# A decoder trunk on one core: queries' parts from one SBUF copy, a filler step behind bare scores, block sums held and spread, first splits in fixed order

## The chip, the core and the metric

The kernel runs on one core of a Trainium2 chip. TensorE (PE in the profile) multiplies, VectorE (DVE) and ScalarE (ACT) here read the PSUM banks into which TensorE writes and write SBUF, GpSimd (POOL) here works from SBUF to SBUF, and SyncE (SP) issues the DMA transfers. Each engine works through its own instructions in order and waits on semaphores for the others. The metric is the device time of one execution in microseconds. A wait of TensorE is named by the instruction that ended it.

## The reference

Two layers act on 1024 tokens of 1024 features, in fp32. Each layer has two token mixers side by side and then a gated feed-forward part with a short causal convolution:

```python
for l in range(DEPTH):                                   # DEPTH = 2
    h = rmsnorm(x, norm1[l])
    proj = h @ w_in[l]                                   # q, k, v of both mixers and the gates
    qa, ka, va, qb, kb, vb, gate_pre = jnp.split(proj, splits, axis=-1)
    o_a = dilated_mixture(hd4(qa, 12), hd4(ka, 12), hd4(va, 12))    # dilated windows, ALiBi, softmax
    o_b = stick_breaking_attention(hd4(qb, 4), hd4(kb, 4), hd4(vb, 4))
    gates = jax.nn.sigmoid(gate_pre + b_gate[l])
    merged = g_a * (o_a @ w_br[l, :OUT_A]) + g_b * (o_b @ w_br[l, OUT_A:])
    x = x + merged @ w_o[l]
    h2 = rmsnorm(x, norm2[l])
    up = h2 @ w_up[l]                                    # 1024 x 5632
    a, v = up[..., :D_FF], up[..., D_FF:]
    a = causal_depthwise_conv(a, conv_w[l], conv_b[l])
    x = x + (jax.nn.gelu(a, approximate=False) * v) @ w_down[l]
return rmsnorm(x, norm_f)
```

Stick-breaking attention of query t over earlier keys s is `sigmoid(z_ts)` times the product of `1 - sigmoid(z_tj)` over the keys j between them. The dilated mixer has three groups of four heads (window 128 at dilation 1, 512 at 4, 2048 at 16), joined by their softmax denominators.

## The kernel before

**Products in parts.** Each operand of a product is split into a rounded high part and the rest. `split` (L128) makes a pair: ScalarE casts the high part (L129), VectorE subtracts it from the source (L130). A product is then three matmuls: high by high, high by low, low by high (L155 to L157). Nearly every operand that reaches TensorE has a pair of L129 and L130 behind it, weights (`w_hi`, `w_lo`) and activations alike.

**Seven products in place of eight.** The large projections (the gates, the dilated groups' keys, queries and values, the feed-forward part) are done by a Strassen-like scheme on 2 x 2 blocks. For it, sums of blocks of the normalised activations are needed in parts: S[1], S[2], S[3] in `t_hi`, `t_lo`, and S[4] in the place of a block of `hh`, `hl`. `block_sums` (L911) writes them as a list of small steps: `first` is three subtractions and additions on POOL (L928 to L930), `further` two on VectorE (L937, L938), `in_two` a split. Each step has a condition, a set of names that must be done first.

**The order of work.** TensorE's instructions stand exactly in the order in which the program writes them (`manual_schedule`, L1870). For the other engines a planner with a model of durations chooses the order within the bounds of the data: when an engine is free in its model it takes the ready instruction that was written first, and so it draws later work ahead of its place if nothing earlier is ready. `high_priority` makes it take an instruction as though it had been written 200 places earlier; the parts of attention weights (`parts`, L593) have it.

**Attention with fillers.** `attend` (L312) walks over a list of items: sixteen of the stick-breaking mixer (B00 to B17), four of the near group (N00 to N11) and sixteen of the two dilated ones (T00 to T17). An item has score steps (TensorE writes `z`, VectorE and ScalarE make weights of it) and pairs of a turn (TensorE transposes the weights, `parts` splits them) and an apply (TensorE multiplies the parts with the values). The steps of one item are mixed with the scores of the next; the last apply of an item, `late`, is written behind the first turn of the next one. Behind each step stands `dense.advance(rate)`: it draws one step of the side list (`aside`, L229) if its condition holds, adds `rate` to a counter, and for each whole one draws a filler, `dense.step()`: six matmuls of a projection. Scores that are left over at an item's end, or that had to wait for their inputs, are written bare, behind one another, each with its `advance`.

The side list holds the block sums. All that is left of it is written at once when the first unit of the seven-product kind is taken up (L262). Keys, queries and values are units of fillers too: `queries_half` (L532) multiplies into a PSUM bank `q_ps`, from which ScalarE takes the high parts of two heads (`qt`, L538; a DMA copies them to the other 64 partitions) and VectorE the low parts (`ql`, L543 and L544). Two banks with the tag `ps` serve all fillers by turns, and two with the tag `s` all scores.

**The opening.** `first` (L1821) loads token blocks of 128 rows, scales them by the norm, transposes them and splits the result into `hh`, `hl`. Between the blocks stand the first projections (`head`, L569): the values' weights come in four loads of 256 KB through two buffers (`wr`), each followed by its split. `masks` (L77) and five small loads (`setup`, L1852) are written ahead of the second block.

**The convolution.** In the feed-forward part `gated` (L1373) makes products of blocks j = 0 and 1; differences of them are taken on POOL (L1382), split and stored (`spill`). The second block's stand between the first ones of the seven-product units `up` (L1489), whose weights are loaded by the same SP queue.

Of the kernel before, what the change touches and what calls it, by code (L numbers as in the profile page):

```python
# [44 lines left out]
AHEAD = 200  # L45

# [6 lines left out]
def trunk_kernel(ctx, tc, x, norm1, w_in, b_gate, w_br, w_o, norm2, w_up, conv_w, conv_b, w_down, norm_f, out, depth=None, probe=None):  # L53
# [74 lines left out]
    def split(hi, lo, src):  # L128
        act.copy(hi, src)  # L129
        dve.tensor_tensor(lo, src, f32(hi), ALU.subtract)  # L130


    def weights(src, cols, place=None):
# [4 lines left out]
        for r in range(0, KD, per):  # L138
            raw = sb.tile([P, per, cols], F32, tag="wr", bufs=NRAW, name="w_raw")
# [55 lines left out]
    class Dense:  # L195
# [58 lines left out]
        def step(self):  # L254
            while True:
                if self.now is None:
# [4 lines left out]
                    if self.now[2] and not self.started:  # L261
                        while self.side:  # L262
                            n = len(self.side)
                            self.aside()
                            assert len(self.side) < n, (self.side, self.done)
# [46 lines left out]
    def attend(dense, items):  # L312
# [4 lines left out]
        for i, (name, first, rest, rate, make) in enumerate(items):  # L317
# [251 lines left out]
    def head(l):  # L569
# [6 lines left out]
        wv = weights(w_in[l][:, OFF_VB : OFF_VB + 256], 256, place(2, "v_w"))  # L576
# [334 lines left out]
    def block_sums(made):  # L911
# [20 lines left out]
        def further(t, a, i):  # L932
# [4 lines left out]
            dve.tensor_tensor(r, f32(ah), r, ALU.subtract)  # L937
            dve.tensor_tensor(r, r, f32(al), ALU.add)  # L938
# [13 lines left out]

        def series(after, t, f, lag, gap):
            steps = {}
            for i in range(4):
                steps.setdefault(i * gap, []).append(lambda i=i: f(i))
                steps.setdefault(i * gap + lag, []).append(lambda i=i: in_two(t, i))
            plan(after, steps)
# [52 lines left out]
    def pair_rest(dense, l, offs, put, view, grid, kept):  # L1011
# [13 lines left out]
        def run():  # L1025
# [47 lines left out]
            yield  # L1073
            for word in seven(pa, w4, S[4], False, True):
# [247 lines left out]
    def ffn(l, pending, final):  # L1322
# [50 lines left out]
        def gated(j, n, v):  # L1373
# [7 lines left out]
            def less(dst, a, b):  # L1381
# [515 lines left out]
```

## Time and profile before

| | |
|---|---|
| median of three runs | 2701.89 us (2699.85 to 2702.15) |
| profiled execution | 2703.52 us |
| its span | 2701.8 us |
| TensorE busy | 2650.5 us (98%) |
| VectorE busy | 2115.7 us (78%) |
| ScalarE busy | 1314.3 us (49%) |
| GpSimd busy | 734.9 us (27%) |
| mean granted clock of TensorE | 0.996 |

The span runs from the first to the last instruction; the profiled execution's own time is 1.7 us longer. An engine's busy time leaves out its waits. Where rows show "[1.28 <-DVE p0l L130]", the engine had been idle for 1.28 us and the instruction of VectorE that writes `p0l` at line 130 released it. Matmuls overlap, so that what a row of several takes is read from the starts.

### The profile page before, as it was taken

To read this page: it belongs to the slowest core of one execution; us is meant where nothing else is said; L and a number is where in the kernel's file an instruction comes from. 1 tells how busy PE (TensorE), PEld (TensorE's weight loads), DVE (VectorE), ACT (ScalarE), POOL (GpSimd) and SP (SyncE) were. 2 spreads that over 40 slices of the span, in tenths; PEclk is the share of its full clock that TensorE was granted. 3 is DMA by queue.
4 is the path that set the end of the run, shared out by engine and by line. 5 is a ranking of instruction groups with operands and counts; after the bars stand their busy time and mean duration, and the time that the engine had idled before them with its cause. 6 is when DMAs were issued, how large, how long until landed. Compare 5 with 4: busy or idle time off the path is not lost. (4 is left out here: it accounts for less than half of the span.)

```text
span 2701.8 us, 37158 instructions
## 1 busy us (share of the span) xinstructions
PE 2650.5 (98%) x13098; PEld 2226.4 (82%) x13098; DVE 2115.7 (78%) x3170; ACT 1314.3 (49%) x2434; POOL 734.9 (27%) x531
## 2 busy tenths in 40 slices
PE   8999999999999999999999999999999999999999
PEld 7888888888888888888889878888788888888888
DVE  5888876675789988897658887766858888998865
ACT  5656544364455555432335655434635555554225
POOL 2004133222233434321120042332311433343210
PEclk9999999999999999999999999999999999999999
DMA  4134489863235444688401334988732443447963
GB/s 153 28 97 125 132 239 234 205 229 118 82 117 172 141 156 143 222 325 313 167 32 48 102 120 145 254 208 226 234 90 75 151 160 135 170 144 254 333 246 121
DMA packets 399559, 448.88 MB, mean 166 GB/s; under 512 B 22044, under 2 KB 319372, under 8 KB 397836
## 3 DMA queue, kind: packets, MB, share of 16 engines
q1 hardware_dynamic: 399372, 446.49, 51.9%
q8 instruction: 104, 1.70, 0.3%
q14 instruction: 83, 0.68, 0.1%
HBM read 300.61 MB, written 142.67 MB: 164 GB/s over the span
## 5 line engine op out<-in xcount | busy, mean ns | idle before, releaser
L130 DVE TENSOR_TENSOR w_lo<-up_a,w_hi 128x512 fp32r<-128x512 f32 x240 | 236.9, 993 | 22.5 <-ACT w_hi L129 22.5
L129 ACT CAST w_hi<-up_a 128x512 fp32r<-128x512 f32 x240 | 149.4, 623 | 186.0 <-PE u_a L906 45.8
L1651 DVE TENSOR_TENSOR x<-x,d_ps 128x512 f32<-128x512 f32 (+1 forms) x228 | 152.3, 672 | 78.0 <-PE d_ps L1645 77.0
L1382 POOL TENSOR_TENSOR cv<-cv 128x512 f32<-128x512 f32 x88 | 131.9, 1509 | 249.0 <-DVE cv L1377 139.1
L130 DVE TENSOR_TENSOR w_lo<-w_raw,w_hi 128x512 fp32r<-128x512 f32 x176 | 133.9, 763 | 64.9 <-ACT w_hi L129 62.3
L129 ACT CAST w_hi<-w_raw 128x512 fp32r<-128x512 f32 x176 | 109.1, 621 | 130.1 <-PE o_ps L156 60.2
L129 ACT CAST w_hi<-in_a 128x512 fp32r<-128x512 f32 x140 | 86.8, 620 | 148.8 <-PE i_a L906 83.4
L130 DVE TENSOR_TENSOR g<-cv,g 128x512 fp32r<-128x512 f32 x154 | 152.3, 990 | 5.2 <-ACT g L129 2.8
L1643 PE MATMUL d_ps<-gd_in,w_hi 128*128 128x512 f32 (+1 forms) x340 | 130.2, 383 | 1.5 <-ACT w_hi L129 1.2
L1645 PE MATMUL d_ps<-gd_in,w_lo 128*128 128x512 f32 (+1 forms) x340 | 129.8, 382 | 0.0
L1644 PE MATMUL d_ps<-gd_in,w_hi 128*128 128x512 f32 (+1 forms) x340 | 129.7, 382 | 0.0
L905 PE MATMUL u_a<-hh,w_hi 128*128 128x512 f32 x320 | 124.7, 390 | 2.7 <-DVE u L1533 2.7
L906 PE MATMUL u_a<-t_lo,w_hi 128*128 128x512 f32 x320 | 124.5, 389 | 0.0
L907 PE MATMUL u_a<-hh,w_lo 128*128 128x512 f32 x320 | 124.5, 389 | 0.0
L905 PE MATMUL u_a<-t_hi,w_hi 128*128 128x512 f32 x320 | 124.5, 389 | 0.0
L906 PE MATMUL u_a<-hl,w_hi 128*128 128x512 f32 x320 | 124.5, 389 | 0.0
L907 PE MATMUL u_a<-t_hi,w_lo 128*128 128x512 f32 x320 | 124.5, 389 | 0.0
L130 DVE TENSOR_TENSOR w_lo<-in_a,w_hi 128x512 fp32r<-128x512 f32 x140 | 115.6, 826 | 3.8 <-ACT w_hi L129 3.5
L1038 POOL TENSOR_TENSOR in_a<-in_a 128x512 f32<-128x512 f32 x28 | 38.0, 1357 | 281.3 <-DVE w_lo L130 281.3
L1643 PE MATMUL d_ps<-gd_in,wd 128*128 128x512 f32 (+1 forms) x292 | 113.9, 390 | 0.0
L129 ACT CAST g<-cv 128x512 fp32r<-128x512 f32 x154 | 94.9, 616 | 38.1 <-POOL cv L1382 29.3
L1645 PE MATMUL d_ps<-gd_in,wd 128*128 128x512 f32 (+1 forms) x292 | 112.8, 386 | 0.0
(395 smaller groups left out, 8706.3 us busy)
## 6 DMA issues: line engine op xcount, KB each, us to landing
gd<-g SPq DMA_DIRECT2D x154, 512.0 KB, 3.6
gd_in<-gd SPq DMA_DIRECT2D x154, 512.0 KB, 6.2
up_a<-in_w_up_dram SPq DMA_DIRECT2D x80, 512.0 KB, 5.7
in_a<-in_w_in_dram SPq DMA_DIRECT2D x56, 512.0 KB, 5.4
w_raw<-in_w_in_dram SPq DMA_DIRECT2D x104, 256.0 KB, 3.4
t_kq<-tk SPq DMA_DIRECT2D x64, 384.0 KB, 7.6
wd_raw<-in_w_down_dram SPq DMA_DIRECT2D x22, 1024.0 KB, 8.0
gin<-gs SPq DMA_DIRECT2D x32, 512.0 KB, 5.2
```

The source lines that it names most:

```text
L129: act.copy(hi, src)
L130: dve.tensor_tensor(lo, src, f32(hi), ALU.subtract)
L905: pe.matmul(o, w[0][:, c], rh, start=(first and i == 0), stop=False, skip_group_check=True)
L906: pe.matmul(o, w[0][:, c], rl, start=False, stop=False, skip_group_check=True)
L907: pe.matmul(o, w[1][:, c], rh, start=False, stop=(last and i == 3), skip_group_check=True)
L1038: pool.tensor_tensor(a11, a22, a11, ALU.subtract)
L1382: return lambda: pool.tensor_tensor(dst, a, b, ALU.subtract)
L1643: pe.matmul(o[:, sub], wh[:, c], gh[:, sub], start=(i == 0 and k in (0, 4, 5)), stop=False, skip_group_check=True)
L1644: pe.matmul(o[:, sub], wh[:, c], gl[:, sub], start=False, stop=False, skip_group_check=True)
L1645: pe.matmul(o[:, sub], wl[:, c], gh[:, sub], start=False, stop=(i == m - 1), skip_group_check=True)
L1651: dve.tensor_tensor(x, x, o[:, sub], ALU.add)
```

## The change

Six edits go together.

1. In the opening the values' weights are loaded by four transfers into one buffer of its own. Their casts stand behind the first token block's casts (ScalarE), their low parts behind the second block's scaling (VectorE), and every second low part is made by POOL. Masks and the small loads are written after the first projections, the masks' VectorE steps behind the last token block. `issue_after(x)` fixes the order behind x for instructions of x's own engine; it adds no semaphore.
2. The last apply of the very first item goes ahead of the second item's first turn (`seq.insert`).
3. Behind each bare score stands one whole filler step in place of an `advance`; it draws no side step and leaves the counter as it is.
4. In the queries that use copies, ScalarE first copies the bank to SBUF, scaled (`q_all`); high and low parts come from there.
5. The VectorE steps of the block sums stand behind the latest low part that was written before them (`behind`). The steps of S[2] go between those of S[1] instead of behind the last item's scores, and those of S[4] come two to a block, are not written at once with the rest, but step by step, and at the latest before the product that reads them.
6. In the convolution's block j = 1 two differences change places, and so do two stores; one difference moves from POOL to VectorE.

```diff
-    def split(hi, lo, src):
+    def split(hi, lo, src, eng=None):
         act.copy(hi, src)
-        dve.tensor_tensor(lo, src, f32(hi), ALU.subtract)
+        return (eng or dve).tensor_tensor(lo, src, f32(hi), ALU.subtract)
+    mark = {}
+    def behind():
+        return tc.issue_after(mark["low"]) if "low" in mark else contextlib.nullcontext()
...
         for r in range(0, KD, per):
+            if place == "opening":
+                if r == 0:
+                    whole = big("wv_raw").rearrange("p a (b c) -> p (a b) c", c=cols)
+                    for q in range(0, KD, per):
+                        nc.sync.dma_start(whole[:, q : q + per, :], src[:, q : q + per, :])
+                hi = sb.tile([P, per, cols], F32R, tag="wh", bufs=4, name="w_hi")
+                lo = sb.tile([P, per, cols], F32R, tag="wl", bufs=4, name="w_lo")
+                with tc.issue_after(mark["hi"]), tc.issue_after(mark["scaled"]):
+                    split(hi, lo, whole[:, r : r + per, :], pool if r // per % 2 else dve)
...
-                        while self.side:
+                        while self.side and self.side[0][0] != LAST_SUM:
...
                 if m == 0 and late:
-                    seq.append(late)
+                    seq.insert(0 if i == 1 else 1, late)
...
                 for f in nxt:
                     f()
-                    dense.advance(rate)
+                    dense.step()
...
         yield from product(o, [(w[k], h_part(n, k)) for k in range(KD)])
+        if copies:
+            whole = small("q_all")
+            act.mul(whole, o, scale)
+            o, scale = whole, 1.0
...
         with tc.high_priority(offset=AHEAD):
-            split(hi[:, :n], lo[:, :n], src[:, :n])
+            mark["low"] = split(hi[:, :n], lo[:, :n], src[:, :n]).ins
...
-            dve.tensor_tensor(r, f32(ah), r, ALU.subtract)
-            dve.tensor_tensor(r, r, f32(al), ALU.add)
+            with behind():
+                dve.tensor_tensor(r, f32(ah), r, ALU.subtract)
+                dve.tensor_tensor(r, r, f32(al), ALU.add)
...
-            split(*S[t][i], at(t, i))
+            with behind():
+                split(*S[t][i], at(t, i))
...
-        series({"N01s"}, 1, lambda i: first(1, b12, b11, i), 7, 6)
-        series({"N11s"}, 2, lambda i: further(2, b22, i), 1, 1)
-        series({"plain", "01", "v0"}, 4, lambda i: further(4, b21, i), 1, 1)
+        steps = {}
+        for i in range(4):
+            for k, f in (
+                (0, lambda i=i: first(1, b12, b11, i)),
+                (7, lambda i=i: in_two(1, i)),
+                (8, lambda i=i: further(2, b22, i)),
+                (10, lambda i=i: in_two(2, i)),
+            ):
+                steps.setdefault(6 * i + k, []).append(f)
+        plan({"N01s"}, steps)
+        steps = {}
+        for i in range(4):
+            steps.setdefault(2 * i, []).append(lambda i=i: further(4, b21, i))
+            steps.setdefault(2 * i + 1, []).append(lambda i=i: in_two(4, i))
+        plan(LAST_SUM, steps)
...
+            while dense.side:
+                dense.aside()
             for word in seven(pa, w4, S[4], False, True):
...
-        if l == 0:
-            masks()
         vectors = setup(l)
-        next(vectors)
+        if l:
+            next(vectors)
...
+        if l == 0:
+            with tc.issue_after(mark["turned"]):
+                masks()
...
-                at(1, less(c12, c, c12))
-                at(1, less(s1, c, s1))
+                pairs = [(2, c12), (1, s1)]
+                if j == 1:
+                    pairs.reverse()
+                for _, t in pairs:
+                    at(1, less(t, c, t))
                 at(later[0], lambda: spill(j, 6, c))
-                at(later[1], lambda: spill(j, 2, c12))
-                at(later[1], less(c, c21, s1))
-                at(later[2], lambda: spill(j, 1, s1))
+                if j > 1:
+                    at(later[1], lambda: spill(j, *pairs[0]))
+                at(later[1], less(c, c21, s1, dve if j == 1 else pool))
+                if j == 1:
+                    at(later[1], lambda: spill(j, *pairs[0]))
+                at(later[2], lambda: spill(j, *pairs[1]))
```

More of the change, by code (lines that the diff above doesn't have):

```diff
@@ L1 @@
+import contextlib
 import concourse.bass as bass
@@ L45 @@
 AHEAD = 200
+LAST_SUM = {"plain", "01", "v0"}
 def f32(ap):
@@ L138, in weights @@
         for r in range(0, KD, per):
+            if place == "opening":
[7 more added lines that the diff above has]
+                    split(hi, lo, whole[:, r : r + per, :], pool if r // per % 2 else dve)
+                got += [(hi[:, i, :], lo[:, i, :]) for i in range(per)]
+                continue
             raw = sb.tile([P, per, cols], F32, tag="wr", bufs=NRAW, name="w_raw")
@@ L574, in place @@
             return x and ([x[0][:, h, :] for h in range(2)] if n == 1 else [y.rearrange("p a b -> p (a b)") for y in x])
-        wv = weights(w_in[l][:, OFF_VB : OFF_VB + 256], 256, place(2, "v_w"))
+        wv = weights(w_in[l][:, OFF_VB : OFF_VB + 256], 256, place(2, "v_w") or "opening")
         wk, wq = (weights(w_in[l][:, off : off + P], P, place(1, "kq_w")) for off in (OFF_KB, OFF_QB))
@@ L951, in plan @@
                 todo.append((after, lambda fs=steps.get(k, ()): [g() for g in fs]))
[L953 to L958, printed above, removed]
         def third(i):
@@ L1379, in gated, with less @@
             later = (2, 3, 4, 5, 7) if j == 1 else (3, 5, 7, 9, 11) if j == NF - 1 else (1, 4, 7, 11, 14)
-            def less(dst, a, b):
-                return lambda: pool.tensor_tensor(dst, a, b, ALU.subtract)
+            def less(dst, a, b, eng=pool):
+                return lambda: eng.tensor_tensor(dst, a, b, ALU.subtract)
             if j % 2 == 0:
@@ L1842, in first @@
                     hd = slice(e0 * P, (e0 + 4) * P)
-                    dve.scalar_tensor_tensor(xr[:, hd], xr[:, hd], ss[:, 2:3], gb[:, hd], ALU.mult, ALU.mult)
+                    scaled = dve.scalar_tensor_tensor(xr[:, hd], xr[:, hd], ss[:, 2:3], gb[:, hd], ALU.mult, ALU.mult)
+                    if (n, c) == (0, 1):
+                        mark["scaled"] = scaled.ins
                     tp = bank("s", "x_t")
@@ L1848, in first @@
                     hi, lo = (h[:, e0 : e0 + 4, c * P : (c + 1) * P] for h in H[n])
-                    split(hi, lo, tv)
+                    made = act.copy(hi, tv)
+                    done = dve.tensor_tensor(lo, tv, f32(hi), ALU.subtract)
+                    if (n, c) == (0, 0):
+                        mark["hi"] = made.ins
+                    mark["turned"] = done.ins
                 yield
```

## The prediction, made before the result was known

> **What bounds the kernel now.** I read the page's busy times first, then who waited for whom on TensorE, then the timeline of every wait of TensorE over 0.5 us.
>
> ```profile
> span 2701.8 us, 37158 instructions
> PE 2650.5 (98%) x13098; PEld 2226.4 (82%) x13098; DVE 2115.7 (78%) x3170; ACT 1314.3 (49%) x2434; POOL 734.9 (27%) x531
> ```
>
> TensorE is busy for 2650.5 of 2701.8 us. The diff adds no matmul and takes none away, and the order in which fillers are drawn only moves them. So the change can only touch the 51.3 us in which TensorE has nothing to run, and stretches where its clock is low. The columns of the next view are: who waited, for whom, us in total, how often, the longest.
>
> ```profile
> PE o L729 <- DVE p0l L130: 10.6, 8, 3.1
> PE x_t L1846 <- issue: 5.2, 1, 5.2
> PE z L590 <- ACT beta L631: 3.2, 6, 1.0
> PE z L590 <- DVE st L813: 3.1, 2, 1.7
> PE u_a L905 <- DVE u L1533: 2.7, 2, 1.6
> PE r_ps L155 <- DVE ql L544: 2.7, 2, 1.4
> PE sb_t L646 <- DVE beta L636: 2.6, 2, 1.3
> ```
>
> The counts are even because the two layers repeat each other. Seven rows hold 30 us; every part of the change stands in front of one of them, except the row of `beta` L631, which it leaves alone.
>
> **Terms of the sum. 1, the opening.** Columns of a timeline: start, us, engine, line, operation, then the idle time before it and what ended it.
>
> ```profile
> 0.00:20.00 20.00, 10.86 (x58) 10.12 (x59) 12.60 (x27) 12.52 (x24) 4.50 (x17) 0.74 0.78 265
> ...
> 9.75 0.16 DVE L1840 RECIPROCAL ss<-ss 128x1 f32<-128x1 f32 x1
> 10.08 0.62 ACT L129 CAST w_hi<-w_raw 128x512 fp32r<-128x512 f32 x1 [0.78 <-DMA w_raw<-in_w_in_dram]
> ...
> 12.54 1.40 DVE L1843 SCALAR_TENSOR_TENSOR xr<-xr,ss,gb 128x512 f32<-128x512 f32 x2
> 13.38 1.94 PE L1846 MATMUL x_t<-ident,xr 128*128 128x128 f32 x8 [5.17 <-issue]
> ```
>
> The second token block could be scaled at 9.91, when its reciprocal is done. It is scaled at 12.54, because ScalarE stood waiting for a weight load that its order put ahead of the first block's casts (10.08), and VectorE queues behind. The transposes at 13.38 need that scaling and the two banks that the first block's low parts release. In the new order the weight splits stand behind the first block's casts on ScalarE and behind the second block's scaling on VectorE, and the seven small mask steps leave VectorE. The earliest start is 9.91 + 0.7 (half of the 1.40) = 10.6; behind the first block's low parts, one step of some 0.7 later, 11.3. That is 2.1 earlier (2.8 at best). Two of four low parts move to POOL, which nothing else needs then, but which may delay VectorE; for that I take off 0.3: **-1.8**. SP issues four more weight transfers (256 KB each) ahead of the third token block: 1 MB at the 265 GB/s of the row is 4 us. That block's turn comes after 24 products of the first block, so I estimate that this is hidden; without that cover it costs up to 3. The five small loads of gains and biases and the mask steps on POOL go behind; their readers come after the whole first product, some 50 us later: nothing. Ends: -4 to +1.
>
> **2, the second stick-breaking item.**
>
> ```profile
> 77.19 0.40 PE L155 MATMUL k_ps<-hh,w_hi 128*128 128x512 f32 x1
> ...
> 78.57 0.27 PE L646 MATMUL sb_t<-ident,beta 128*128 128x128 f32 x1
> 80.14 0.44 PE L646 MATMUL sb_t<-ident,beta 128*128 128x128 f32 x2 [1.31 <-DVE beta L636]
> ```
>
> A filler step is six matmuls, 77.19 to 78.57, 1.38 us. Ahead of this wait the change puts the first item's apply (some 0.5 us) and, by the step behind the bare score, a filler that would have come later. Together that covers 1.31. Of 2.6 in both layers I take **-2.3** (ends -2.6 and 0: the filler may come one place too late).
>
> **3, queries.**
>
> ```profile
> 179.79 1.21 ACT L538 ACTIVATE qt<-q_ps 64x512 fp32r<-64x512 f32 x2
> ...
> 184.34 0.69 DVE L544 SCALAR_TENSOR_TENSOR ql<-q_ps,qt 64x512 fp32r<-64x512 f32 x1
> ...
> 185.18 0.47 PE L155 MATMUL r_ps<-hh,w_hi 128*128 128x512 f32 x1 [1.36 <-DVE ql L544]
> ```
>
> The bank is free when VectorE's second low part is through, 5 us after ScalarE began. With one copy to SBUF it is free at about 180.4, so the wait goes: 2.7 in both layers. The price is one more ScalarE pass in each of 12 halves, about 0.6 each (the 1.21 is two passes), 7 us of an engine that is busy 49%. What waits behind it are the casts of the attention parts, which are on TensorE's path; I charge a fifth, 1.3. The copies of the two halves on SP go out 0.6 later, for scores that come items later: nothing. Net **-1.4**, ends -2.7 and +3. The low parts now read two SBUF tensors, which is priced as a rival.
>
> **4, block sums.**
>
> ```profile
> 269.35 1.28 DVE L937 TENSOR_TENSOR h_sum<-hh,h_sum 128x512 f32<-128x512 f32 x2
> 270.55 0.68 DVE L130 TENSOR_TENSOR w_lo<-w_raw,w_hi 128x512 fp32r<-128x512 f32 x1
> 271.15 0.68 DVE L938 TENSOR_TENSOR h_sum<-h_sum,hl 128x512 f32<-128x512 f32 x1
> 271.75 0.68 DVE L130 TENSOR_TENSOR p0l<-t,p0h 128x512 fp32r<-128x512 f32 x1
> ...
> 272.49 0.38 PE L729 MATMUL o<-p0l,v 128*128 128x256 f32 x1 [3.06 <-DVE p0l L130]
> ```
>
> Three block-sum steps, which the planner drew far ahead of their place, and a weight split stand ahead of the low part that TensorE needs. `behind()` forbids just this: a sum step cannot pass the latest low part written before it. The eight waits of this kind make 10.6. Weight splits are not held (0.68 each here), and a step that is released may still stand in front of the next low part; I leave 0.4 for each wait, 3.1 in all: **-7.5**, ends -10.6 and 0. The hold is an order on VectorE alone; casts and POOL's sums go as before. Held steps are late next for the first block-summed product; by my count of the loop about 22 of the 29 steps of the first two sums are drawn by then, and the last sum's eight fall on the nine steps behind. Only the rest is forced; this is the first rival.
>
> **5, far items.**
>
> ```profile
> 416.00:426.00 10.00, 8.54 (x40) 7.04 (x39) 7.29 (x16) 4.46 (x11) 4.78 (x3) 0.83 1.08 295
> ...
> 420.45 0.33 PE L590 MATMUL z<-t_kq 128*128 128x128 f32 x1 [1.46 <-DVE st L813]
> ...
> 421.98 0.63 PE L905 MATMUL i_c<-t_hi,w_hi 128*128 128x512 f32 x1
> ...
> 424.11 0.63 PE L907 MATMUL i_c<-t_hi,w_lo 128*128 128x512 f32 x1
> ```
>
> Two items' scores follow each other with no filler, and the second waits for its banks. A filler step of 1.38 fits into 1.46. So of 3.1 I take -2.9. Behind the wait six matmuls take 0.63 and start 0.43 apart (421.98 to 424.11) where such a step otherwise runs at 0.23, at a granted clock of 0.83 over the ten us: 1.2, with the short scores ahead 1.6, and the same in the other layer if its wait does the same. The Trainium skill, "TensorE: Matmul & The Clock Gate", Part 1, says that the gate looks at a free-running window of about 3.4 us and halves the clock after an idle one; the trace agrees in the length of the slow stretch, but a wait of 3.06 left the clock alone, so whether a window is hit is luck. By that rule the clock's part would be 0 to 3.4 in a given execution. From the rows I take 2.2 of 3.2. Together **-5.1**, ends -6.3 and -1.
>
> **6, the convolution's second block.**
>
> ```profile
> 776.39 0.62 ACT L129 CAST w_hi<-up_a 128x512 fp32r<-128x512 f32 x1 [5.19 <-DMA up_a<-in_w_up_dram]
> ...
> 778.48 0.47 PE L905 MATMUL u_a<-hh,w_hi 128*128 128x512 f32 x1 [1.13 <-DVE u L1533]
> ```
>
> The wait named for VectorE goes back to a load that landed late, queued on SP behind the stores of the spilled parts. The swap of two differences, with one on VectorE in place of POOL, brings those stores forward by half a us or so: **-0.8** of 2.7, ends -2.7 and +1.
>
> **7.** The planner places everything anew round the moved steps, and some waits like the six of `beta` (3.2) will come up that are not there now: **+1.9**, ends 0 and +5.
>
> Sum: -1.8 - 2.3 - 1.4 - 7.5 - 5.1 - 0.8 + 1.9 = **-17.0**. The profiled execution took 2703.52 us, 1.7 beyond its span; the median of the runs is 2701.89. Taken off the median: **2685**.
>
> **Rivals. A, held too long: slower.**
>
> ```profile
> L938 DVE TENSOR_TENSOR h_sum<-h_sum,hl 128x512 f32<-128x512 f32 x8 | 7.6, 954 | 0.0
> ```
>
> If the held steps are still undone when the first block-summed product starts, they run in front of it: 16 VectorE steps of about 0.95 (this row) are 15 us per layer, less some 3 that two fillers cover: 12 per layer, +24 - 17 = +7, **2709**. For it speaks that each step is now chained to the next low part; against it, that about 40 attention steps lie between. It decides from about 12 steps left.
>
> **B, the hold does not hold.** What the planner moves ahead may be the casts and weight splits, and term 4 gives nothing: -9.5, **2692**.
>
> **C, low parts that collide with POOL.**
>
> ```profile
> 70.00:240.00 170.00, 164.43 (x982) 143.39 (x981) 147.48 (x263) 103.99 (x230) 6.19 (x6) 1.00 0.27 80
> 240.00:340.00 100.00, 94.73 (x501) 79.13 (x500) 84.45 (x158) 57.74 (x135) 39.91 (x28) 1.00 0.41 124
> ...
> 264.97 1.61 POOL L1034 TENSOR_TENSOR in_a<-in_a 128x512 f32<-128x512 f32 x1
> 265.68 1.45 DVE L130 TENSOR_TENSOR w_lo<-w_raw,w_hi 128x512 fp32r<-128x512 f32 x1
> ```
>
> A subtraction of two SBUF tensors took 1.45 beside POOL's step and 0.68 alone (270.55). With the copy in SBUF, 24 low parts become such. If all collided, 24 x 0.77 = 18 us of VectorE; on the path, near the casts, perhaps a third: 6, so **2691**. But POOL works 6.19 of 170 us where eight of the twelve halves are, and 39.91 of 100 where the other four are. "SBUF — State Buffer" of the Trainium skill, Who interferes with whom, says that a VectorE instruction with two SBUF inputs contends with a GpSimd instruction that reads SBUF, the later one being blocked, and speaks against this part; the two durations agree with it.
>
> **D, no change:** new waits eat the gain: three to four times the upper end of term 7 leave about **2700**.
>
> **How the numbers follow.** Forecast 0.62 (all seven terms about as above), B 0.15, C 0.09, D 0.06, A 0.08. Two tenths of a per cent, 5.4 us, is about what a measurement of this kernel can tell from no change. The forecast, B and C are faster: 0.86; D the same: 0.06; A slower: 0.08. The forecast's own range is 2677 to 2691, from -25 (terms 1, 4 and 6 near their good ends) to -11 (term 4 at half, term 7 at +4). With B, C and part of D it reaches to 2697; below, 2675.
>
> **What would show it.** Term 1: the transposes of the second block near 11.3, not 13.38. Term 2: no wait on `beta` L636 in TensorE's waits. Term 3: none on `ql` L544. Term 4: the row of `p0l` near 3 in place of 10.6, and no new wait at the first `i_a` products for `t_lo` (that would be A). Term 5: none on `st` L813, and no stretch of 0.63 us matmuls. Term 6: `u` L1533 under 2.7. The prediction is wrong if TensorE's idle time does not fall to some 36 us, or if its busy time rises.

## The result: slower, 2713.1 us

| | before | after |
|---|---|---|
| median (six runs each) | 2701.67 us (2699.85 to 2702.15) | 2713.14 us (2711.10 to 2717.86) |
| ratio | | 1.0042, 95% interval 1.0031 to 1.0052 |
| profiled execution | 2703.52 us | 2711.98 us |

The forecast was 2685, a gain of 17 us; the change costs 11.5. The page of the changed kernel, span and busy times (the PE in `x13098` is the same number of matmuls):

```profile
span 2710.2 us, 37153 instructions
PE 2657.2 (98%) x13098; PEld 2228.5 (82%) x13098; DVE 2102.5 (78%) x3170; ACT 1320.1 (49%) x2446; POOL 737.7 (27%) x531
```

TensorE's busy time rose by 6.7 us with the same matmuls, so part of them ran at a low clock. Its idle time, which was to fall to some 36 us, went from 51.3 to 53.0. Who waited for whom on TensorE, with the same columns as before:

```profile
PE i_a L928 <- ACT t_hi L132: 9.0, 2, 5.1
PE i_a L928 <- ACT hh L132: 4.6, 2, 2.7
PE o L752 <- ACT p0h L132: 3.3, 2, 1.8
PE z L613 <- ACT beta L654: 3.0, 6, 0.7
PE x_t L1887 <- DVE xr L1882: 2.8, 1, 2.8
PE z L613 <- DVE st L731: 2.7, 2, 2.3
```

The rows that the change aimed at are gone or small: none on `ql`, none for `sb_t` on `beta`, and `p0l`, 10.6 before, has left the top of the list. (The matmul helper, L155 to L157 before, is now L174 to L176, and `split` is L132 and L133.) At the top stand two waits per layer of `i_a`, the seven-product units, for parts of block sums: `t_hi`, and `hh` in the case of S[4]. That is the place that rival A names. The timeline of the first one, with start, us, engine, line:

```profile
317.15 0.54 DVE L133 TENSOR_TENSOR p0l<-t,p0h 128x384 fp32r<-128x384 f32 x1
...
317.62 1.30 DVE L133 TENSOR_TENSOR t_lo<-h_sum,t_hi 128x512 fp32r<-128x512 f32 x1
317.67 0.39 PE L930 MATMUL i_a<-t_hi,w_lo 128*128 128x512 f32 x1
318.85 1.28 DVE L961 TENSOR_TENSOR h_sum<-hh,h_sum 128x512 f32<-128x512 f32 x2
320.05 1.28 DVE L962 TENSOR_TENSOR h_sum<-h_sum,hl 128x512 f32<-128x512 f32 x2
320.76 0.62 ACT L132 CAST hh<-h_sum 128x512 fp32r<-128x512 f32 x1 [4.66 <-DVE h_sum L962]
321.36 0.62 ACT L132 CAST t_hi<-h_sum 128x512 fp32r<-128x512 f32 x1
...
322.03 0.80 PE L928 MATMUL i_a<-t_hi,w_hi 128*128 128x512 f32 x1 [3.97 <-ACT t_hi L132]
...
326.56 0.63 PE L930 MATMUL i_c<-t_hi,w_lo 128*128 128x512 f32 x1
```

To be read from the bottom up. TensorE has had three of the four blocks of the second sum by 318.1 and waits 3.97 us for the cast of the fourth. The cast waits for the update of that block (L961, L962), this for the low part of the first sum in the same tile (317.62), and all of it stands, by the hold, behind the low part `p0l` of 317.15. The updates come in pairs, one of S[2] and one of S[4], so that the late chain is nearly twice as long. ScalarE idles 4.66. Behind the wait TensorE's matmuls take 0.63 until 327, half the clock. By stretches of time (busy us with the counts of PE, PEld, DVE, ACT, POOL; then granted clock, DMA share and GB/s):

```profile
316.00:346.00 30.00, 22.57 (x101) 17.40 (x100) 25.57 (x37) 9.71 (x20) 8.26 (x6) 0.89 0.18 53
...
1660.00:1700.00 40.00, 31.57 (x145) 24.92 (x144) 32.56 (x50) 13.74 (x27) 8.87 (x6) 0.91 0.33 94
```

The same in both layers: TensorE idle for over 7 of 30 and 8 of 40 us, at a granted clock of 0.89 and 0.91. A table by stages shows that this is the whole loss. Each entry is the time between the first matmuls (or the first and last) of the names given, in us, both layers added; the last two columns are two experiments that come below. Each column is one profiled execution.

| stage, from the starts of TensorE's matmuls | before | after | e13 | e16 |
|---|---|---|---|---|
| keys and first items: `pt_c` to next `v_ps` | 71.6 | 67.5 | 67.5 | 70.5 |
| stick-breaking items: to the first `t` | 281.6 | 283.5 | 284.9 | 278.6 |
| near group: to the first `i_a` | 155.2 | 151.7 | 151.3 | 152.9 |
| first to last `i_a` | 505.7 | 521.7 | 504.1 | 503.0 |
| first to last `u_a` | 764.5 | 762.4 | 761.4 | 761.3 |
| the rest of the span | 923.1 | 923.4 | 924.2 | 922.4 |

The `i_a` stage costs 16.0, all the others together bring 7.6. (With edit 3 four short matmuls per layer go from the first stage to the second, about 0.7 us for both layers, and four from the third to the fourth, about 0.9.)

### The profile page after: what moved, and what is told of

Read it like the earlier page. It is cut to its first block, busy times and chain, and to the rows that moved or that the text cites. A ratio compares the mean times of both kernels' runs of the same rounds, so it can differ in the third digit from the quotient of the medians.

```text
span 2710.2 us, 37153 instructions
## 1 busy us (share of the span) xinstructions
PE 2657.2 (98%) x13098; PEld 2228.5 (82%) x13098; DVE 2102.5 (78%) x3170; ACT 1320.1 (49%) x2446; POOL 737.7 (27%) x531
## 5 line engine op out<-in xcount | busy, mean ns | idle before, releaser
L133 DVE TENSOR_TENSOR w_lo<-up_a,w_hi 128x512 fp32r<-128x512 f32 x240 | 237.5, 996 | 20.1 <-ACT w_hi L132 20.1
L132 ACT CAST w_hi<-up_a 128x512 fp32r<-128x512 f32 x240 | 149.4, 622 | 184.2 <-PE u_a L929 45.4
L133 DVE TENSOR_TENSOR w_lo<-w_raw,w_hi 128x512 fp32r<-128x512 f32 x172 | 130.3, 761 | 62.9 <-ACT w_hi L132 59.6
L132 ACT CAST w_hi<-in_a 128x512 fp32r<-128x512 f32 x140 | 86.7, 619 | 159.6 <-PE i_a L929 84.3
L132 ACT CAST w_hi<-w_raw 128x512 fp32r<-128x512 f32 x172 | 106.9, 622 | 116.8 <-PE o_ps L175 61.3
L133 DVE TENSOR_TENSOR g<-cv,g 128x512 fp32r<-128x512 f32 x154 | 150.3, 977 | 5.2 <-ACT g L132 2.7
L133 DVE TENSOR_TENSOR w_lo<-in_a,w_hi 128x512 fp32r<-128x512 f32 x140 | 112.5, 804 | 6.8 <-ACT w_hi L132 6.2
L1682 PE MATMUL d_ps<-gd_in,wd 128*128 128x512 f32 (+1 forms) x292 | 113.9, 390 | 0.0
L132 ACT CAST g<-cv 128x512 fp32r<-128x512 f32 x154 | 94.9, 616 | 38.1 <-POOL cv L1416 30.1
L1684 PE MATMUL d_ps<-gd_in,wd 128*128 128x512 f32 (+1 forms) x292 | 112.8, 386 | 0.0
L1683 PE MATMUL d_ps<-gd_in,wd 128*128 128x512 f32 (+1 forms) x292 | 112.8, 386 | 0.0
```

Of the source, the lines that this page charges most:

```text
L133: return (eng or dve).tensor_tensor(lo, src, f32(hi), ALU.subtract)
L1682: pe.matmul(o[:, sub], wh[:, c], gh[:, sub], start=(i == 0 and k in (0, 4, 5)), stop=False, skip_group_check=True)
L1683: pe.matmul(o[:, sub], wh[:, c], gl[:, sub], start=False, stop=False, skip_group_check=True)
L1684: pe.matmul(o[:, sub], wl[:, c], gh[:, sub], start=False, stop=(i == m - 1), skip_group_check=True)
```

## Experiments

No kernel here leaves any of the computation out. The ratios are to the kernel before, run on the same chip by turns, with 95% intervals. The prediction speaks of about 22 side steps drawn; that was my estimate. Counted in the program, the changed kernel has drawn 24 of the 29 steps of its list when the first seven-product unit is taken up; of the five that are then written at once, three do something: the split of S[1]'s fourth block (index 25), the update of S[2]'s (26) and its split (28).

**Which part carries the loss: e1 to e4.** e1 undoes edit 5; e2 keeps the new lists and lets the hold go:

```diff
 def behind():
-    return tc.issue_after(mark["low"]) if "low" in mark else contextlib.nullcontext()
+    return contextlib.nullcontext()
```

e3 keeps the hold and brings the three old `series` and the old "all at once" back:

```diff
-                        while self.side and self.side[0][0] != LAST_SUM:
+                        while self.side:
...
+        series({"N01s"}, 1, lambda i: first(1, b12, b11, i), 7, 6)
+        series({"N11s"}, 2, lambda i: further(2, b22, i), 1, 1)
+        series({"plain", "01", "v0"}, 4, lambda i: further(4, b21, i), 1, 1)
```

e4 lets a bare score draw a side step again, beside its filler:

```diff
                 for f in nxt:
                     f()
+                    dense.aside()
                     dense.step()
```

> The changed kernel with all of edit 5 undone: no hold, the old three lists of block sums, all of the last one written when the first seven-product unit starts. If late block sums cost the time, the 9.0 us of waits of i_a for t_hi and the 4.6 for hh go, the p0l waits come back (8 to 10 us in place of 1.5), and the time is 2692 to 2700 us. If the loss sits in another edit, it stays at 2708 us or more.

> The changed kernel with the hold alone taken away (the VectorE steps of the sums may be drawn ahead again); the new list stays. Theory 1, that the new list draws the steps of S[2] and S[4] too late: the waits of i_a for t_hi and hh stay above 6 us in total and the time within 4 us of 2713. Theory 2, that the hold makes them late: those waits fall below 3 us, the p0l waits rise above 6, the time is 2704 us or less.

> The changed kernel with the hold kept and the old three lists put back, all forced at the first seven-product unit. Theory 1 (the list): i_a waits under 3 us in total, 2700 us or less. Theory 2 (the hold): i_a waits of 9 us or more, since more steps are forced at once and none may go ahead; 2710 us or more.

> The changed kernel in which each bare score draws one side step again besides its filler: four more of the 29 steps are drawn before the first seven-product unit. Theory 1: the steps of S[2]'s last part come in time, the t_hi wait falls from 9.0 to under 3 us, and the time to 2700 to 2706. Theory 2: drawn earlier but held as before, 2710 us or more.

| | median, us | ratio | interval |
|---|---|---|---|
| e1, edit 5 undone | 2698.64 | 0.9982 | 0.9972 to 0.9992 |
| e2, no hold | 2697.64 | 0.9979 | 0.9969 to 0.9988 |
| e3, hold with the old lists | 2711.33 | 1.0032 | 1.0020 to 1.0044 |
| e4, side steps at bare scores | 2697.57 | 0.9980 | 0.9969 to 0.9990 |

TensorE's waits in e3, the kernel with the hold and the old lists:

```profile
PE i_a L928 <- ACT t_hi L132: 10.5, 3, 5.2
PE i_a L928 <- DVE u L1076: 4.4, 2, 2.2
```

and in e4, with four more side steps drawn at the near group's bare scores:

```profile
PE i_a L930 <- DVE hl L133: 4.3, 2, 2.6
...
PE o L753 <- ACT p0h L132: 2.9, 2, 1.5
```

Without the hold the loss is gone whatever the lists (e1, e2): the planner then draws the late steps ahead, as it did before. With the hold it stays, with the old lists too (e3). So the new lists are not what costs by themselves. But the hold alone isn't either: e4 keeps it whole, and four more draws bring some 16 us. e1 and e2 have 8.2 and 8.5 us of waits on `p0l`, which the hold was made against, and come out where e4 does.

**What the single parts are worth: e5 to e8.** e5, e6 and e7 are the kernel before with one edit each: the opening (1), the queries (4), the filler step behind bare scores (3). e8 is e4 without edit 4.

```diff
-        if copies:
-            whole = small("q_all")
-            act.mul(whole, o, scale)
-            o, scale = whole, 1.0
```

> The kernel before with edit 1 alone. Prediction's term 1: the second block's transposes near 11.3 us, the whole 1 to 2 us faster than before. Rival: the earlier start is used up by a later token block or by the clock, and the time is the same within 0.5 us.

> The kernel before with edit 4 alone. Prediction's term 3: the wait on ql goes (2.7 us), 1.3 come back, net 1 to 2 us faster. Rival (price of the extra ScalarE pass): the casts p0h and sbh come late, new waits of 2 to 4 us on them, and with a lowered clock behind one of them the kernel is as fast as before or up to 4 us slower.

> The kernel before with edit 3 alone (a filler step behind each bare score, no side step drawn there). With the old lists unheld the missing draws should cost nothing. Terms 2 and 5: the waits of z for st L813 fall from 3.1 to under 1 and the slow stretches behind them go, 3 to 6 us faster. If the missing draws cost by themselves, a wait of i_a of over 2 us appears and the kernel is not faster.

> The run with a side step at each bare score (2697.6 us), and edit 4 undone as well. If ScalarE's extra pass is what makes p0h late, the waits of o for p0h (2.9 us, with lowered clock behind them) go, the wait on ql comes back (2.7), and the time is 2694 to 2697. If p0h is late for another reason, they stay and the time rises to 2698 to 2702.

| | median, us | ratio | interval |
|---|---|---|---|
| e5, opening alone | 2700.95 | 0.9993 | 0.9985 to 1.0002 |
| e6, queries alone | 2698.47 | 0.9982 | 0.9973 to 0.9991 |
| e7, filler step alone | 2709.38 | 1.0019 | 1.0010 to 1.0027 |
| e8, e4 with the old queries | 2706.67 | 1.0011 | 1.0003 to 1.0020 |

TensorE's waits in e7, the filler step alone:

```profile
PE o L748 <- DVE p0l L133: 10.1, 6, 3.6
...
PE r_ps L174 <- DVE ql L563: 4.3, 4, 1.4
PE u_a L924 <- DVE u L1556: 3.8, 2, 2.1
```

Edit 3, for which term 5 had a gain of 5.1, costs 5 when it stands alone. Its expectation had it 3 to 6 us faster, or not faster with a wait of `i_a` of over 2 us; it is slower, and there is no such wait. Part of what it aimed at happened (the far items' wait on `st` is 1.8 in e7 in place of 3.1, and the clock stays up behind it in both layers), but every filler behind is now one place on, and four waits on `ql` stand where two were, `u` rose by 1.1, and slow stretches that the kernel before does not have follow at 275, 1364, 1524 and 1617 us. e8 shows the other side: with the old queries e4's gain is gone, and the same four waits on `ql` are there. Between the ratios of e4 and e8 lie 0.0031, 8.4 us. So edit 4 brings 4.6 alone and 8.4 beside edit 3: it takes away the very waits that edit 3 makes more of.

The price of edit 4 that term 3 charges, late casts of the attention parts, is not there. ScalarE is busy for 5.8 us more in the changed kernel, but without the copy the waits on `p0h` do not go: they are 2.8 in e8 and 2.9 in e4, so the first theory of e8 falls, and its time is above the ranges of both. They come with the hold: every kernel with it has 2.2 or more, every kernel without it 0.7 or less. ScalarE, VectorE and TensorE of the changed kernel in layer 1:

```profile
1607.83 0.62 ACT L132 CAST t_hi<-h_sum 128x512 fp32r<-128x512 f32 x1 [4.48 <-POOL h_sum L953]
...
1608.88 0.59 ACT L557 ACTIVATE q_all<-q_ps 128x512 f32<-128x512 f32 x1
1609.37 0.58 ACT L132 CAST p0h<-t 128x512 fp32r<-128x512 f32 x1
```

```profile
1610.59 0.79 DVE L566 SCALAR_TENSOR_TENSOR ql<-q_all,qt 64x512 fp32r<-64x512 f32 x1
1611.41 1.66 DVE L567 SCALAR_TENSOR_TENSOR ql<-q_all,qt 64x512 fp32r<-64x512 f32 x1
```

```profile
1610.00 0.38 PE L752 MATMUL o<-p0h,v 128*128 128x256 f32 x1 [1.80 <-ACT p0h L132]
...
1611.33 0.63 PE L174 MATMUL r_ps<-hh,w_hi 128*128 128x512 f32 x1
...
1613.46 0.63 PE L176 MATMUL r_ps<-hh,w_lo 128*128 128x512 f32 x1
```

ScalarE stands idle for 4.48 us until GpSimd has finished a block sum, casts it (`t_hi`), and that cast, a weight's and the copy all stand ahead of the `p0h` for which TensorE waits 1.80 us. The copy is 0.5 of it, but in e8 the first pass of `qt` stands in the same place. How the hold moves `t_hi` there is not shown. Six matmuls behind run at half clock. One low part took 1.66, the other 0.79: rival C's collision with POOL, which is at work from 1610.91 (a step of 1.61), is there, but behind the path.

**The hold or the place: e9 to e12.** e9 is the changed kernel with edit 3 undone, so that bare scores draw as they did. e10 sets the blocks of the list closer, so that its last steps come earlier:

```diff
-                steps.setdefault(6 * i + k, []).append(f)
+                steps.setdefault(5 * i + k, []).append(f)
```

e11 is e4 with S[4] as before (five steps, all written at the first seven-product unit, not held); e12 is e11 with `4 * i + k`.

> The changed kernel with edit 3 alone undone: behind a bare score stands an advance again, with its side step and its rate. If the late draws of held steps are the cause, the waits of i_a for t_hi fall from 9.0 to under 3 us and the time to 2696 to 2702; the two waits of z for st L836 behind bare far scores come back (2 to 3 us). If the hold is enough to make the sums late by itself, 2708 us or more.

> The changed kernel with the four parts of S[1] and S[2] five side steps apart in place of six, so that the list is three steps shorter and nothing else differs. If it is the number of steps still undrawn when the first seven-product unit starts, the t_hi waits fall from 9.0 to under 3 us and the time to 2697 to 2703. If the bare scores' side step works in another way (its place), the waits stay over 6 us and the time over 2708.

> The run with a side step at each bare score (2697.6 us) and S[4] as it was before: five steps, all written when the first seven-product unit starts, and not held. The waits of i_a for hl (4.3 us) go; what comes back is at most the two p0l waits of 0.7 and 0.2 per layer that the kernel before had there. 2693 to 2696 us. If VectorE is simply full there, it stays within 1 us of 2697.6.

> As the run before, with the parts of S[1] and S[2] four side steps apart: drawn eight steps earlier than in the changed kernel's list. If late draws were all, nothing is left to gain and the time is within 1 us of the run before; if denser steps crowd the low parts again, the p0l waits rise above 4 us and it is 2 to 4 us slower.

| | median, us | ratio | interval | on `t_hi`, us |
|---|---|---|---|---|
| e9, edit 3 undone | 2702.88 | 1.0003 | 0.9995 to 1.0012 | none (7.5 on `hh`) |
| e10, 5 steps between blocks | 2712.81 | 1.0038 | 1.0026 to 1.0051 | 8.7 |
| e11, e4, S[4] at once | 2704.86 | 1.0005 | 0.9996 to 1.0014 | 7.1 |
| e12, e11 with 4 steps | 2698.11 | 0.9984 | 0.9975 to 0.9993 | none (5.4 on `w_lo`) |

In e9 the wait on `t_hi` goes, as expected, but `hh` takes its place and the time is 0.9 us above the range: S[4]'s last block is late there, and in layer 0 three steps of VectorE just ahead of its cast take 1.60 to 1.77 us beside GpSimd's steps (from 329 us on), where such a step takes 0.68 alone. So rival C's collision, though with other steps than the low parts it had in mind, does stand on the path of this kernel.

e10 was a miss for the theory of a mere count: three steps fewer in the list, only one left over, and the same wait. VectorE of e10 shows why:

```profile
314.14 0.82 DVE L133 TENSOR_TENSOR t_lo<-h_sum,t_hi 128x512 fp32r<-128x512 f32 x1
316.80 1.12 DVE L133 TENSOR_TENSOR w_lo<-in_a,w_hi 128x512 fp32r<-128x512 f32 x1 [1.84 <-ACT w_hi L132]
...
319.63 0.54 DVE L133 TENSOR_TENSOR p0l<-t,p0h 128x384 fp32r<-128x384 f32 x1
320.10 1.27 DVE L961 TENSOR_TENSOR h_sum<-hh,h_sum 128x512 f32<-128x512 f32 x2
321.30 1.27 DVE L962 TENSOR_TENSOR h_sum<-h_sum,hl 128x512 f32<-128x512 f32 x2
```

The update of the fourth block could have run at 315, when `t_lo` is through; VectorE even idles for 1.84 us. But it was the last step drawn (index 23; 24 are drawn), and so it is tied to the low part of the very turn that stands before the first product, at 319.63. How many steps are left over is not what decides, but how far ahead of this last low part the update is written. e11 and e12 both went against their expectations: e11 is 7 us slower than e4 in place of faster or the same, e12 is 7 faster than e11. In e11 S[4], written all at once and free of the hold, stands on VectorE ahead of the last update (its `hl` takes 1.78 us at 316.75), and `t_hi` is late again; that this is the cause was not tested apart. e12 moves the list ahead and `t_hi` isn't late.

**The same with the rest of the change whole: e13 to e16.** e13 is the changed kernel with one digit replaced; e14 has S[4]'s steps behind one another besides; e15 is the changed kernel without edits 3 and 5; e16 is e13 with edit 3 undone.

```diff
-                steps.setdefault(6 * i + k, []).append(f)
+                steps.setdefault(4 * i + k, []).append(f)
...
-            steps.setdefault(2 * i, []).append(lambda i=i: further(4, b21, i))
-            steps.setdefault(2 * i + 1, []).append(lambda i=i: in_two(4, i))
+            steps.setdefault(i, []).append(lambda i=i: further(4, b21, i))
+            steps.setdefault(i + 1, []).append(lambda i=i: in_two(4, i))
```

> The changed kernel with the blocks of the first two sums 4 steps apart in place of 6. Counted in the program, 24 steps of this list are drawn before the first seven-product unit in the changed kernel; its list has 29, the last update of S[2] is the 27th and is written with the rest, two places too late. With 5 apart it was the 24th and so the last one drawn, and t_hi was as late. With 4 apart it is the 21st and has three more draws behind it. Theory (the place decides; the hold is harmless once three or so steps lie between): no wait on t_hi over 1 us in either layer, 9.0 us and some 5 of half clock go, the wait on hh of 4.6 stays: about 2699. Rival (the hold itself makes the last sums late, wherever they are written): t_hi stays at 7 or more, 2710 to 2713.

> As the last one, and the last sum's steps one behind the other (five steps in place of eight, still held). Theory (S[4] is late because its steps are spread so far that the last of them stand too near its product): the wait on hh falls from 4.6 to under 2, time 2 to 4 us under the last kernel, about 2696. Rival (it is the hold behind the low parts that makes it late): hh stays at 4 or more and the time is that of the last kernel.

> The changed kernel without edits 3 and 5: the opening, the second item, the queries and the convolution's block. Theory (edits 3 and 5 are the only ones that cost): under both the kernel with edit 5 undone (0.9982) and the one with the queries alone (0.9982), by what the opening, the second item and the convolution bring, 1.7 + 4.1 (two layers) + 2: 2690 to 2695, 0.996 to 0.9975. Rival (the small edits are given back by clock drops and new waits elsewhere): 2697 to 2700.

> The changed kernel with edit 3 undone and 4 steps between the blocks. With edit 3 undone alone the list was empty at the first unit and the time 2702.88; its wait was on hh, 7.5 us. Theory (its t_hi was early already, so the shorter list brings nothing there): hh stays at 5 or more, 2700 to 2704. Rival (steps of S[2] still undone are what S[4] waits for): hh falls under 3 and the time to 2696.

| | median, us | ratio | interval |
|---|---|---|---|
| e13, 4 steps between blocks | 2696.60 | 0.9980 | 0.9972 to 0.9989 |
| e14, and S[4] in five steps | 2693.75 | 0.9970 | 0.9959 to 0.9982 |
| e15, without edits 3 and 5 | 2696.53 | 0.9975 | 0.9966 to 0.9985 |
| e16, e13 without edit 3 | 2693.51 | 0.9965 | 0.9952 to 0.9977 |

TensorE's waits in e13:

```profile
PE i_a L929 <- DVE hl L133: 3.2, 2, 1.6
...
PE o L752 <- ACT p0h L132: 2.9, 2, 1.5
```

and in e16:

```profile
PE o L752 <- DVE p0l L133: 4.6, 9, 1.1
PE z L613 <- ACT beta L654: 3.0, 6, 0.7
...
PE z L613 <- DVE st L836: 2.3, 3, 1.5
```

One digit turns the change from 11.5 us slower to 6.1 faster, with the hold as it is. `t_hi` is no longer among the waits, and the table of stages above shows where it comes from: the `i_a` stage of e13 takes 504.1 in place of 521.7, the others stay within 1.4. The last update of S[2] in e13, in the place where the changed kernel is late:

```profile
310.70 0.28 DVE L133 TENSOR_TENSOR p0l<-t,p0h 128x128 fp32r<-128x128 f32 x1
...
311.71 0.68 DVE L961 TENSOR_TENSOR h_sum<-hh,h_sum 128x512 f32<-128x512 f32 x1
...
312.42 0.69 DVE L962 TENSOR_TENSOR h_sum<-h_sum,hl 128x512 f32<-128x512 f32 x1
...
313.14 0.62 ACT L132 CAST t_hi<-h_sum 128x512 fp32r<-128x512 f32 x1
...
315.29 0.48 PE L928 MATMUL i_a<-t_hi,w_hi 128*128 128x512 f32 x1
```

It stands behind an earlier low part, and the cast is through 1.5 us before the first product. So the theory of the place holds, and the one that blames the hold wherever the steps stand falls. In e14 `i_a` has no wait on `hh` or `hl` either, so S[4] was late by its place too; its 2.9 us over e13 is less than the two intervals can tell apart. In the same stretches as above, e14:

```profile
316.00:346.00 30.00, 28.03 (x142) 22.99 (x141) 27.08 (x45) 12.53 (x26) 8.27 (x6) 1.00 0.40 116
1660.00:1700.00 40.00, 38.94 (x182) 32.12 (x181) 33.79 (x50) 15.64 (x31) 14.83 (x11) 1.00 0.66 191
```

e16 went against its theory and with its rival: the shorter list brings much there too (by the ratios 10 us under e9). S[4] is made in the same tile as S[2] and its steps follow in the same list, so they come up earlier with it: the last update of S[4] in layer 0 starts at 324.41 us in place of 330.75, and the wait on `hh` of 7.5 is gone. e15 lies between its two theories. e14 and e16 are the fastest of all the kernels, 9 us under the kernel before.

## Why the prediction was wrong

**The step that failed** stands in term 4: "Held steps are late next for the first block-summed product; by my count of the loop about 22 of the 29 steps of the first two sums are drawn by then ... Only the rest is forced", with rival A's "It decides from about 12 steps left". The count was near enough (24), but the sum has nothing for the rest. In the runs the three steps that are left cost 9.0 us of waits on `t_hi` and, with S[4] behind them, 4.6 on `hh` and stretches at half clock: 16.0 us in the `i_a` stage, which e13 gets back by their place alone. The threshold was wrong: I priced the held steps by their sum on VectorE, 16 steps of 0.95, and asked how many of them would have to be left. What decides is one chain, the last block's: low part, two updates, cast, tied to the last low part ahead. With 24 drawn three steps were left; with e10 only one, and the wait was the same. In the changed kernel the update of the last block came three places too late to be drawn, in e10 it was the last one drawn; with one draw behind it 1.5 us are left on `t_hi` (e4), with three nothing (e13). That "about 40 attention steps lie between" was no argument, since the list was spaced to use them up. And I left out that edit 3 takes away draws on the way: I wrote that a bare score "draws no side step" and did not subtract the four of the near group from the list's lead. With them 28 of the 29 steps are drawn (e4). Rival A is what happened, in the place that it names and in its direction, 2709 for 2713. That the number is so near is luck: its 24 us were 16.0, with the half clock in them that it left out, and the gain of 17 that it set against them was 7.6.

**The rest of the sum was too large as well.** With the late steps out of the way the same edits bring 6 us (e13) to 9 (e14), not 17, and no kernel's median here is in the range of the forecast. Both signs of being wrong that the prediction names are there: the idle time did not fall, and the busy time rose.

**Term 4** itself did what it says: waits on `p0l` in the changed kernel fell from 10.6 to 1.5, waits on `p0h` of 3.3 came instead, so 5.8 of the 7.5 in waits. In time it is worth less: e16 is 3.0 under e15, which differs also by the lists, and e2, with 8.5 on `p0l`, is as fast as e4. By the table of stages the near group, where the longest of these waits are, gains 3.5 in the changed kernel, about 0.9 of it by matmuls that went to the next stage. By the same measure e4 is 8.7 shorter than e2 in the near group (151.4 and 160.1) and 5.1 longer in the `i_a` stage (505.9 and 500.8), in one execution of each: much of what the hold gains is handed on to the next stage.

**Term 1** (-1.8): right. The second block's transposes, in the changed kernel:

```profile
9.58 1.42 DVE L1882 SCALAR_TENSOR_TENSOR xr<-xr,ss,gb 128x512 f32<-128x512 f32 x2
...
11.65 1.97 PE L1887 MATMUL x_t<-ident,xr 128*128 128x128 f32 x8 [2.35 <-DVE hl L1891]
```

They start at 11.65 (forecast 11.3) in place of 13.38, and the first `pt_c`, where the stages above begin, at 65.08 in place of 66.65. e5 has -2.1 by its medians, with an interval that holds zero.

**Term 2** (-2.3): the wait is gone. Of the 4.1 us by which the first stage is shorter, about 0.7 are the matmuls that went to the next stage. The order alone leaves 1.8 of the wait for `sb_t` (e15, e16), the filler step alone all 2.6 (e7); only both together cover it.

**Term 3** (-1.4): right in its mechanism, too small. Alone it is -4.6, with an interval of -7.3 to -2.4 that holds the 2.7 of the wait without the 1.3 taken off: e6 has no wait on `p0h`. Beside edit 3 it is -8.4: there four waits on `ql` make 4.3 us, and in e8 stretches at half clock start at 181.9, 270.6, 1519.9 and 1612.0 us, each within 0.6 us of the end of one of them.

**Term 5** (-5.1): wrong in sign for the edit as a whole, +5 alone (e7). The wait went as told, 3.1 to 1.1 in the changed kernel, and the slow stretches at 422 and 1760 us too. (Two filler steps of 1.38 could cover 2.8 of it, not the 2.9 that was taken.) What went wrong is term 7's +1.9 for the waits that come up anew when every filler moves by a place; for edit 3 alone, with the old queries, they and their slow stretches came to some 10, if the 5.1 was gained and 5 were lost on balance; this is a difference, not a measurement of its own. With the new queries the edit costs little: e13 is 3.1 over e16, and the intervals overlap.

**Term 6** (-0.8): not shown. The `u_a` stage is 2.1 shorter, but there is no experiment of its own, and without edit 6 the wait on `u` there goes from 0.5 (e5) to 3.8 (e7). In the changed kernel rival C was there in single rows and off the path; B and D did not occur.

## What to carry to other kernels

An order that forbids a planner to work ahead hands its lead back to the place where the work is written: look at the last link in the chain that the first reader needs, and count how far behind the last fixed point it stands, not how much is left in sum. Where two loops feed from one counter (here the bare scores and the side list), changing what one step draws changes the lead of the other. And when every filler moves by one place, expect waits to be traded, not removed: a change that takes the longest wait of the next coincidence away first (here the queries) made the shift cheap.

## What the runs showed of the hardware

A wait on TensorE can cost more than its length, and how much more depends on when it falls. In the kernel before, the wait of 3.06 us at 272.5 left the clock alone. In e5, the same wait of the same length:

```profile
271.19 0.58 PE L748 MATMUL o<-p0l,v 128*128 128x256 f32 x1 [3.06 <-DVE p0l L133]
...
274.14 0.63 PE L176 MATMUL r_ps<-hh,w_lo 128*128 128x512 f32 x1
```

The matmuls that took 0.39 to 0.40 take 0.63 there. By the trace's record of the clock all such stretches between the opening and the end are 3.41 us long or twice that, in all eighteen kernels, and 3.41 us at half the clock are up to 1.7 us lost. Within a trace their starts lie whole multiples of 3.413 us apart (320.76, 1610.99 and 1665.61 in the changed kernel: 378 and 16 of them), as though the clock were set anew window by window. The Trainium skill, "TensorE: Matmul & The Clock Gate", Part 1, gives the length of the window as about 3.4 us and says that it runs free, which agrees with both the length and the spacing.

In these windows the two waits differ. The columns are the stretch, its length, TensorE's busy time, its clock, and the share and rate of the DMA; first the kernel before, then e5:

```profile
267.60:271.01 3.41, 1.83 (x10) 1.00 0.39 115
271.01:274.43 3.42, 1.95 (x10) 1.00 0.53 161
```

```profile
266.68:270.09 3.41, 1.45 (x7) 1.00 0.40 115
270.09:273.50 3.41, 2.31 (x7) 0.50 0.59 193
```

In the kernel before the wait is split over two windows, which leaves 1.6 and 1.5 us idle; in e5 one window has 1.96, and the next is at half the clock. In the eighteen traces, from 25 to 2660 us, there are 36 windows at full clock with 1.95 us or more in which no matmul runs, and half the clock follows on every one; with 1.40 to 1.94 idle on 14 of 52; below that on 10 of some 13,700, all ten near 1360 us at the border of the layers. So what looks like chance is in the main how a wait falls on the windows, which no edit here controls. The same section of the Trainium skill lets the clock fall after an idle window; here 1.80 us of waiting with short matmuls around it were enough (1610.00 above, 2.1 us idle in its window).

The runs of one kernel spread by 2 to 12 us, more than most terms of the sum. The changed kernel's spread by 6.8: 2711.10 at a mean granted clock of 0.996, 2717.86 at 0.994.
